# Upper halves of 30 weight tiles of a decoder layer: from ScalarE's rounding to a rounding transfer of GpSimd's

## The chip, the cores and the metric

The kernel runs on one core of a Trainium2 chip. The metric is the device time of one execution in microseconds (us), as a median of several runs. Engines are TensorE (PE), VectorE (DVE), ScalarE (ACT), GpSimd (POOL) and SyncE (SP); each works through its own instructions one after the other in the order in which they stand in the program, and waits at an instruction until what it needs is there.

## What is computed

One layer of a hybrid decoder, on x of 512 positions by 1024 channels, in float32. Cut to what matters:

```python
proj = rmsnorm(x, norm_gain) @ w_in
aq, ak, av, ag, bq, bf, bi, bg, gate_a, gate_b = split(proj)      # 8 of 512 columns, 2 of 1024
ya = moba_attention(rmsnorm(aq), rmsnorm(ak), av, rel_bias)      # 8 heads of 64
ya = (ya * silu(ag)) @ w_up_a
log_f = log_sigmoid(bf) + log1p(lb * exp(min(-bf, 30)))
kb = (1 - lb) * sigmoid(-bf)
yb = rmsnorm(hgrn2_chunkwise(silu(bq), kb, bi, log_f))           # 4 heads of 128
yb = (yb * silu(bg)) @ w_up_b
h = x + (sigmoid(gate_a) * ya + sigmoid(gate_b) * yb) @ w_out
out = h + (p @ w_ple) * sigmoid(h @ w_ple_gate)
```

The input projection is by far the largest product. The attention works on four pairs of heads, the recurrence on four heads.

## The kernel before

**Products in three passes.** A float32 product is made from halves: each operand v is held as an upper half, v rounded to the format fp32r that TensorE multiplies, and a lower half, the rest v − upper, and the product is upper·upper + upper·lower + lower·upper (`mm3`, lines 289 to 295). A weight tile of 128 partitions by 1024 columns holds 8 blocks of 128 channels for 128 outputs, so one tile is 24 matmuls into one PSUM bank.

**Weights.** `w_sequence` lists all weight tiles in the order of use. For each tile `w_load` (lines 258 to 267) brings the raw floats from DRAM to `wf`; from tile 10 on GpSimd issues these transfers (line 266). `w_split` makes the upper half `wh` on ScalarE (line 276), and the lower half `wl` on VectorE (line 277), which reads the raw tile and the upper half. `weight` (lines 280 to 287) is called where a tile is used and lets loads and splits run two tiles ahead. There are two raw buffers, three of `wh` and three of `wl` (line 97): the upper half of tile i takes the buffer of tile i−3, which is free once TensorE has done that tile; the raw tile i takes the buffer of tile i−2, which is free once VectorE has made that one's lower half.

Tiles 0 to 17 are those of the token-major projections and of the first head's `bf` and `bq`. Tiles 18 to 47 are the 30 of `w_tr`, 1024 columns each: the gates `bg` (recurrence) and `ag` (attention), the forget gate `bf` and the query `bq` of recurrence heads 1 to 3, and the merge gates `ga` (gate_a) and `gb`. The ones that are spoken of below: 18 is `bg0`, 19 `ag0`, 20 `bf1`, 21 `bq1`, 22 `bg1`, 23 `ag1`, 26 `bq2`, 25 `bf2`, 32 `bf3`, 37 `ag3`, 39 `ga1`. Behind them come the up-projections (narrower tiles), `w_o` and `w_g`.

**Order.** TensorE's instructions stand in the order of the code, written by hand (`ENG`). In the first part of the kernel those of ScalarE, VectorE and SyncE do too; from the attention on a scheduler places them by its own estimates of when each is ready, and with it the rows of GpSimd's queue.

**Banks.** PSUM has eight banks: three (`mm`) go round among the products of `mm3`, the outputs of the attention and the third score tile of a step; three (`a`) hold scores; two (`g`) serve the recurrence (line 102). A product can begin when what was in its bank three `mm` uses earlier has been read. What reads them last is VectorE: `silu_block` multiplies the gate by its sigmoid (L491, `bg0s` to `bg3s` and `ag0s` to `ag3s`); `hgrn_gates` computes the recurrence's decays from `bf` (L512 to L523, the last a scan over four pieces) and multiplies the query with its sigmoid (L526, the last read of `bq`); `softmax` adds the position bias to the scores and takes their maximum (L832, on `s00x`, `s20x` and so on for a third score tile in an `mm` bank), then ScalarE takes the exponential (L834), VectorE the reciprocal of the sum (L835), ScalarE scales (L836) and VectorE transposes (L839). SyncE then sorts the transposed blocks by transfers (L850) and loads the next pair's bias (L880). In `qk_norm` queries and keys are transposed by L759 and pass through DRAM (`kthere`).

Of the kernel before, what the change touches and what calls it, by code (L numbers as in the profile page):

```python
# [14 lines left out]
AF = mybir.ActivationFunctionType  # L15
# [5 lines left out]
KD = D // 128  # L21
# [28 lines left out]
WAIT = 16  # L50
# [18 lines left out]
def hybrid_layer_kernel(  # L69
# [17 lines left out]
    V, A, G, PE = nc.vector, nc.scalar, nc.gpsimd, nc.tensor  # L87
# [11 lines left out]
    def unit(tag, name, dt=F32, shape=(128, 512)):  # L99
        return sb.tile(list(shape), dt, tag=tag, bufs=BUFS[tag], name=name)  # L100
# [132 lines left out]
    wseq, wraw, wtile, wpos, rounds = [], [], [], [0], {}  # L233
    late = []
# [23 lines left out]
    def w_load(upto):  # L258
        while len(wraw) <= min(upto, len(wseq) - 1):
            ap, kn, cols = wseq[len(wraw)]  # L260
            if len(wraw) >= late[0] or len(wraw) in EARLY:
                raw = unit("VV", f"wf{len(wraw)}", shape=(128, 2, 512)).rearrange("p a b -> p (a b)").rearrange(
                    "p (k c) -> p k c", k=kn)
            else:
                raw = unit("w", f"wf{len(wraw)}", shape=(128, kn, cols))
            (G if len(wraw) >= FAR else nc.sync).dma_start(raw, ap)  # L266
            wraw.append(raw)

    def w_split(upto):
        while len(wtile) <= min(upto, late[1] - 1):  # L270
            i = len(wtile)
            w_load(i)
            ap, kn, cols = wseq[i]
            hi = unit("wh", f"wh{i}", R, (128, kn, cols))
            lo = unit("wl", f"wl{i}", R, (128, kn, cols))
            rounds[i] = A.activation(hi, wraw[i], AF.Copy)  # L276
            V.tensor_tensor(lo, wraw[i], hi.bitcast(F32), op=OP.subtract)  # L277
            wtile.append((hi, lo))

    def weight(ap, ahead=LD):  # L280

        i = wpos[0]
        wpos[0] += 1
        assert wseq[i][0] is ap or str(wseq[i][0]) == str(ap), i
        w_load(i + ahead + (LATE if i + ahead + LATE >= late[0] else 0))
        w_split(i + ahead)
        return wtile[i]
# [631 lines left out]
    def start(kp):  # L919

        if kp == 0:
# [23 lines left out]
            load_x(6, KD)  # L945
            x_gain(2, 3)
            w_split(2)
        elif kp == 1:
            x_gain(3, 4)
            x_square(0)  # L950
            x_square(1)
            x_gain(4, 5)
            w_load(4)
            w_split(3)
            x_square(2)
            x_gain(5, 6)
# [23 lines left out]
    ya, yb, qn, kn, sags, sbgs = [], [], [], [], [], []  # L980
# [365 lines left out]
```

## Time and profile before

| | |
|---|---|
| median of 3 runs | 453.32 us (452.07 to 454.05) |
| the profiled execution | 452.42 us, its span 450.6 us |
| TensorE busy | 445.8 us, 99% |
| VectorE busy | 334.6 us, 74% |
| ScalarE busy | 289.7 us, 64% |
| GpSimd busy | 59.9 us, 13% |
| bytes moved | 59.53 MB, 132 GB/s over the span |

A row of groups reads: line of the program, engine, operation, output<-inputs with their shape, x count, then busy us and the mean ns of one, then the idle us of the engine ahead of these instructions and what ended most of it. A timeline row: start and duration in us from the span's start, engine, line, operation, and in brackets the idle time before it with its releaser. A DMA row: KB of one and the us from issue to landing. A row of windows: for each engine the busy time in the window and its instructions, then the granted TensorE clock (1.00 is full), the mean share of the 16 DMA engines that is busy, and GB/s.

### The profile page before, as it was taken

How to read it: one execution, taken by the hardware profiler on the slowest of the kernel's cores; microseconds unless marked ns; L12 is line 12 of the kernel's file. 1: busy time of each engine (PE TensorE's matmuls, PEld its weight loads, DVE VectorE, ACT ScalarE, POOL GpSimd, SP SyncE). 2: the span in 40 equal slices, each digit the busy share in tenths (PEclk: the TensorE clock that was granted, in tenths of full speed). 3: DMA queues.
4: the chain of work that ended last, by engine and by line, in shares of the span. 5: the costliest groups of instructions: out<-in, count | busy, mean ns of one | idle time of the engine just before them, and what ended most of it. 6: DMA issues, size and time to landing. Idle time of an engine off the chain costs nothing.

```text
span 450.6 us, 8536 instructions
## 1 busy us (share of the span) xinstructions
PE 445.8 (99%) x3192; PEld 376.2 (83%) x3192; DVE 334.6 (74%) x682; ACT 289.7 (64%) x561; POOL 59.9 (13%) x97
## 2 busy tenths in 40 slices
PE   9999999999999999999999999999999999999996
PEld 8888888888878888878887888878888888899996
DVE  5869494776899797949857775465479868999844
ACT  5958474746689988979857996784135434555421
POOL 1000100000000101010100000111210103325520
PEclk9999999999999999999999999999999999999999
DMA  8802424168594455171425444265551444312111
GB/s 265 317 1 94 141 93 129 48 219 197 167 215 127 159 134 178 46 203 49 142 93 155 140 135 148 70 197 149 184 173 47 168 145 143 129 47 95 49 47 48
DMA packets 32857, 59.53 MB, mean 132 GB/s; under 512 B 7088, under 2 KB 18736, under 8 KB 32816
## 3 DMA queue, kind: packets, MB, share of 16 engines
q0 software_dynamic: 9056, 32.51, 22.5%
q1 hardware_dynamic: 23616, 26.47, 20.4%
q8 instruction: 25, 0.41, 0.4%
q14 instruction: 16, 0.13, 0.1%
q10 hardware_dynamic: 144, 0.01, 0.0%
HBM read 48.74 MB, written 4.98 MB: 119 GB/s over the span
## 4 chain that ended last, share of the span: by engine, by line
PE 89%; DVE 5%; SPq 2%; DMA 1%; issue 1%; ACT 0%; DVEq 0%
PE h L293 10%; PE g L1210 9%; PE ga L293 9%; PE gb L293 7%; PE ub L293 5%; PE aq L423 5%; PE ak L423 5%; PE ua L293 5%; PE av L423 5%; PE bf L293 5%; PE bi L423 5%; PE bq L293 4%; PE bg L293 4%; PE ag L293 4%; PE pe L293 2%; SPq L850 2%
## 5 line engine op out<-in xcount | busy, mean ns | idle before, releaser
L276 ACT ACTIVATE wh<-wf 128x1024 fp32r<-128x1024 f32 (+1 forms) x70 | 67.0, 958 | 63.2 <-issue 9.8
L277 DVE TENSOR_TENSOR wl<-wf,wh 128x1024 fp32r<-128x1024 f32 (+1 forms) x70 | 76.8, 1097 | 38.0 <-ACT wh L276 35.7
L266 POOL DMA_DIRECT2D wf<-in_w_tr_dram x30 | 15.8, 528 | 170.5 <-DVE wl L277 115.4
L293 PE MATMUL ga<-xh,wh 128*128 128x512 f32 x64 | 25.3, 396 | 0.4 <-DVE bg3s L491 0.4
L293 PE MATMUL gb<-xh,wh 128*128 128x512 f32 x64 | 25.0, 391 | 0.0
L293 PE MATMUL ga<-xh,wl 128*128 128x512 f32 x64 | 24.9, 390 | 0.0
L293 PE MATMUL ga<-xl,wh 128*128 128x512 f32 x64 | 24.9, 389 | 0.0
L293 PE MATMUL gb<-xl,wh 128*128 128x512 f32 x64 | 24.9, 389 | 0.0
L293 PE MATMUL h<-mh,wh 128*128 128x512 f32 x64 | 24.9, 389 | 0.0
L293 PE MATMUL h<-ml,wh 128*128 128x512 f32 x64 | 24.9, 389 | 0.0
L293 PE MATMUL h<-mh,wl 128*128 128x512 f32 x64 | 24.9, 389 | 0.0
L293 PE MATMUL gb<-xh,wl 128*128 128x512 f32 x64 | 24.9, 389 | 0.0
L834 ACT ACTIVATE pb<-pb,ps 128x128 f32<-128x128 f32 (+3 forms) x32 | 17.6, 551 | 10.0 <-DVE ps L832 10.0
L832 DVE CUSTOM_DVE_ANT_0 pb<-s,bias 128x128 f32<-128x128 f32 (+3 forms) x28 | 12.8, 493 | 7.1 <-DMA bias<-in_ed_dram 4.8
L1187 ACT ACTIVATE sg<-sg 128x256 f32<-128x256 f32 x12 | 5.0, 414 | 20.2 <-DVE sg L1184 20.2
L836 ACT ACTIVATE pb<-pb,ps 128x128 f32<-128x128 f32 (+3 forms) x32 | 16.0, 550 | 0.0
L542 ACT ACTIVATE hx<-hx 128x512 f32<-128x512 f32 x24 | 14.9, 623 | 1.4 <-DVE hx L541 1.3
L266 POOL DMA_DIRECT2D wf<-in_w_up_dram x16 | 8.6, 538 | 52.2 <-DVE wl L277 32.2
L839 DVE STREAM_TRANSPOSE pb<-pb 128x512 f32<-128x512 f32 x20 | 13.8, 696 | 2.0 <-ACT pb L836 2.0
L266 POOL DMA_DIRECT2D wf<-in_w_tok_dram x8 | 4.4, 549 | 80.2 <-DVE wl L277 68.2
L293 PEld LDWEIGHTS ga<-xh,wh 128*128 128x128 f32 x64 | 12.0, 188 | 3.5 <-DVE bg3s L491 0.8
L293 PEld LDWEIGHTS ga<-xh,wl 128*128 128x128 f32 x64 | 12.0, 188 | 2.6
(958 smaller groups left out, 1434.9 us busy)
## 6 DMA issues: line engine op xcount, KB each, us to landing
wf<-in_w_tr_dram POOLq DMA_DIRECT2D x30, 512.0 KB, 4.2
wf<-in_w_tok_dram POOLq DMA_DIRECT2D x8, 512.0 KB, 3.6
wf<-in_w_up_dram POOLq DMA_DIRECT2D x16, 256.0 KB, 3.0
wf<-in_w_o_dram POOLq DMA_DIRECT2D x8, 512.0 KB, 3.8
wf<-in_w_g_dram POOLq DMA_DIRECT2D x8, 512.0 KB, 3.6
wf<-in_w_tok_dram SPq DMA_DIRECT2D x6, 512.0 KB, 7.6
pb<-pb SPq DMA_DIRECT2D x64, 48.0 KB, 2.9
bias<-in_ed_dram SPq DMA_DIRECT2D x8, 256.0 KB, 4.1
```

The costliest lines, as they stand in the source:

```text
L266: (G if len(wraw) >= FAR else nc.sync).dma_start(raw, ap)
L276: rounds[i] = A.activation(hi, wraw[i], AF.Copy)
L277: V.tensor_tensor(lo, wraw[i], hi.bitcast(F32), op=OP.subtract)
L293: dense.append(PE.matmul(ps, a[:, k, :], b[k], start=(n == 0), stop=(n == tot - 1)))
L423: dense.append(PE.matmul(banks[t], a[:, s_], b[:, kk, :], start=(k == 0 and i == 0), stop=(k == KD - 1 and i == 2)))
L542: A.activation(x, x, AF.Exp)
L832: in_order(V.tensor_tensor_reduce(p_, s_[:, so:so + nk], T[j][:, nk - 1::-1], -1.0, 3e38, OP.add, OP.min, st[:, 0:1]))
L834: A.activation(p_, p_, AF.Exp, bias=st[:, 0:1], scale=-1.0, accum_out=st[:, 1:2])
L836: A.activation(p_, p_, AF.Copy, scale=st[:, 2:3])
L839: V.transpose(z[:, :, b_, :].rearrange("p b (n c) -> p b n c", c=32), pb[:, b_].rearrange("p (n b c) -> p b n c", b=4, c=32))
L850: nc.sync.dma_start(pt[32 * b:32 * b + 32, a], z[32 * a:32 * a + 32, b])
L1210: dense.append(PE.matmul(dst[i], a[:, k], b, start=(m == 0 and i in (1, 6, 5)), stop=(m == 11), skip_group_check=i not in (1, 6, 5)))
```

## The change

For tiles 18 to 47 (`WAIT` is 16, `late[0]` the place of the first `w_o` tile; `kn == KD` leaves out the narrow ones and so what follows tile 47 ahead of `w_o`) the upper half no longer comes from ScalarE reading the raw tile. GpSimd issues a second transfer of the same weights from DRAM, straight into the upper half's buffer, whose type is fp32r, so that the transfer rounds. The raw tile is loaded as before and the lower half is computed as before.

```diff
             hi = unit("wh", f"wh{i}", R, (128, kn, cols))
             lo = unit("wl", f"wl{i}", R, (128, kn, cols))
-            rounds[i] = A.activation(hi, wraw[i], AF.Copy)
+            if WAIT < i < late[0] and kn == KD:
+                G.dma_start(hi, ap)
+            else:
+                rounds[i] = A.activation(hi, wraw[i], AF.Copy)
             V.tensor_tensor(lo, wraw[i], hi.bitcast(F32), op=OP.subtract)
             wtile.append((hi, lo))
```

`rounds[WAIT]`, to which `qk_norm` ties an operation, is that of tile 16 and stays as it was. Lines behind 276 are three higher in the changed kernel: L277 is L280, L491 is L494, L526 is L529, L832 is L835. TensorE's order is the same in both. ScalarE's loses 30 rows. GpSimd's gets 30 transfers `wh`, each waiting for its buffer, with the raw loads between and behind them. VectorE's has the same operations, but the scheduler has moved the `wl` rows back.

On VectorE, at the decays of recurrence head 1 (`hu1`, `ha1`, `hk1`; `kl0` is a key's lower half), before:

```order
L277 TENSOR_TENSOR wl23_1288<-wf23_1285,wh23_1287 128x1024
L512 TENSOR_SCALAR hu1_1324<-bf1_1249 128x512
L231 SCALAR_TENSOR_TENSOR kl0_1134<-ktp_1274,sm_68,kh0_1130 128x512
L515 SCALAR_TENSOR_TENSOR ha1_1320<-bf1_1249,ha1_1320 128x512
L517 TENSOR_TENSOR hk1_1329<-ha1_1320,bf1_1249 128x512
L519 TENSOR_TENSOR ha1_1320<-ha1_1320,hu1_1324 128x512
L523 SCALAR_TENSOR_TENSOR hu1_1324<-onec_86,ha1_1320 128x128 x4
L618 TENSOR_TENSOR hkd1_1750<-hu1_1324 128x384
L277 TENSOR_TENSOR wl24_1344<-wf24_1341,wh24_1343 128x1024
```

and now:

```order
L515 TENSOR_SCALAR hu1_1324<-bf1_1249 128x512
L231 SCALAR_TENSOR_TENSOR kl0_1134<-ktp_1274,sm_68,kh0_1130 128x512
L518 SCALAR_TENSOR_TENSOR ha1_1320<-bf1_1249,ha1_1320 128x512
L520 TENSOR_TENSOR hk1_1329<-ha1_1320,bf1_1249 128x512
L522 TENSOR_TENSOR ha1_1320<-ha1_1320,hu1_1324 128x512
L526 SCALAR_TENSOR_TENSOR hu1_1324<-onec_86,ha1_1320 128x128
L280 TENSOR_TENSOR wl23_1288<-wf23_1285,wh23_1287 128x1024
L526 SCALAR_TENSOR_TENSOR hu1_1324<-onec_86,ha1_1320 128x128 x3
L621 TENSOR_TENSOR hkd1_1750<-hu1_1324 128x384
```

`wl23` stood ahead of the decays and stands between the first scan and the other three now, and `wl24` stands further back.

Shortly behind, on VectorE, the bias is added to the first scores (`s00x` is the third score tile, in an `mm` bank) and the query `ha1` is made from `bq1`; before:

```order
L620 TENSOR_TENSOR hkd1_1750<-hkd1_1750,hk1_1329 128x384
L526 TENSOR_TENSOR ha1_1320<-ha1_1320,bq1_1291 128x512
L543 TENSOR_TENSOR hx1_64_1352<-hk1_1329,hx1_64_1352 128x4x64
L622 STREAM_TRANSPOSE hkt1_1754<-hkd1_1750 128x384
L832 ISA pb_70,ps000_1386<-s000_1364,bias00_1307 128x128
L832 ISA ps000_1386 128x1
L832 ISA pb_70,ps001_1391<-s001_1365,bias01_1309 128x128
L832 ISA ps001_1391 128x1
L832 ISA pb_70,ps010_1396<-s002_1366,bias00_1307 128x256
L832 ISA ps010_1396 128x1
L832 ISA pb_70,ps011_1401<-s00x_1367,bias01_1309 128x256
```

and now:

```order
L835 ISA pb_70,ps001_1391<-s001_1365,bias01_1309 128x128
L835 ISA ps001_1391 128x1
L835 ISA pb_70,ps010_1396<-s002_1366,bias00_1307 128x256
L835 ISA ps010_1396 128x1
L835 ISA pb_70,ps011_1401<-s00x_1367,bias01_1309 128x256
L835 ISA ps011_1401 128x1
L835 ISA pb_70,ps020_1407<-s000_1364,bias00_1307 128x384
L835 ISA ps020_1407 128x1
L835 ISA pb_70,ps021_1413<-s001_1365,bias01_1309 128x384
L835 ISA ps021_1413 128x1
L529 TENSOR_TENSOR ha1_1320<-ha1_1320,bq1_1291 128x512
```

The query's row, the last read of the bank of `bq1`, stood ahead of all the score rows and stands behind them now.

On VectorE in the last score step of the second pair (`s110`, `s111`) with the decays of recurrence head 3; before:

```order
L277 TENSOR_TENSOR wl34_2185<-wf34_2182,wh34_2184 128x1024
L277 TENSOR_TENSOR wl35_2216<-wf35_2213,wh35_2215 128x1024
L832 ISA pb_70,ps130_2231<-s110_2223,bias10_1861 128x512
L832 ISA ps130_2231 128x1
L832 ISA pb_70,ps131_2237<-s111_2224,bias11_1863 128x512
L832 ISA ps131_2237 128x1
L512 TENSOR_SCALAR hu3_2411<-bf3_2188 128x512
L515 SCALAR_TENSOR_TENSOR ha3_2407<-bf3_2188,ha3_2407 128x512
L835 RECIPROCAL ps130_2231<-ps130_2231 128x1
```

and now:

```order
L280 TENSOR_TENSOR wl34_2185<-wf34_2182,wh34_2184 128x1024
L835 ISA pb_70,ps130_2231<-s110_2223,bias10_1861 128x512
L835 ISA ps130_2231 128x1
L835 ISA pb_70,ps131_2237<-s111_2224,bias11_1863 128x512
L835 ISA ps131_2237 128x1
L515 TENSOR_SCALAR hu3_2411<-bf3_2188 128x512
L518 SCALAR_TENSOR_TENSOR ha3_2407<-bf3_2188,ha3_2407 128x512
L280 TENSOR_TENSOR wl35_2216<-wf35_2213,wh35_2215 128x1024
L838 RECIPROCAL ps130_2231<-ps130_2231 128x1
```

`wl35` stood ahead of the score rows and stands between the decays and the reciprocal of the softmax now.

On GpSimd, at tiles 21 to 25; before:

```order
L266 DMA wf21_1207<-in_w_tr_dram 128x1024
L266 DMA wf22_1243<-in_w_tr_dram 128x1024
L266 DMA wf23_1285<-in_w_tr_dram 128x1024
L266 DMA wf24_1341<-in_w_tr_dram 128x1024
L266 DMA wf25_1472<-in_w_tr_dram 128x1024
```

and now:

```order
L266 DMA wf21_1207<-in_w_tr_dram 128x1024
L266 DMA wf22_1243<-in_w_tr_dram 128x1024
L277 DMA wh21_1209<-in_w_tr_dram 128x1024
L277 DMA wh22_1245<-in_w_tr_dram 128x1024
L266 DMA wf23_1285<-in_w_tr_dram 128x1024
L277 DMA wh23_1287<-in_w_tr_dram 128x1024
L266 DMA wf24_1341<-in_w_tr_dram 128x1024
L277 DMA wh24_1343<-in_w_tr_dram 128x1024
L266 DMA wf25_1472<-in_w_tr_dram 128x1024
```

Each upper half's transfer stands in the queue ahead of the raw load of the next tile or the one after it.

## Prediction

> **What bounds the kernel now.** I read the page's busy totals first, then its costliest groups, then the busy time of each engine in the stretch where the 30 changed tiles are used, then what ends the waits. From the page:
>
> ```profile
> PE 445.8 (99%) x3192; PEld 376.2 (83%) x3192; DVE 334.6 (74%) x682; ACT 289.7 (64%) x561; POOL 59.9 (13%) x97
> ...
> L276 ACT ACTIVATE wh<-wf 128x1024 fp32r<-128x1024 f32 (+1 forms) x70 | 67.0, 958 | 63.2 <-issue 9.8
> L277 DVE TENSOR_TENSOR wl<-wf,wh 128x1024 fp32r<-128x1024 f32 (+1 forms) x70 | 76.8, 1097 | 38.0 <-ACT wh L276 35.7
> L266 POOL DMA_DIRECT2D wf<-in_w_tr_dram x30 | 15.8, 528 | 170.5 <-DVE wl L277 115.4
> ```
>
> TensorE is busy 99% of the span of 450.6 us. VectorE idles 35.7 us ahead of its `wl` operations because the upper half is not there yet: so the upper half's arrival already paces VectorE. The stretch of the changed tiles, and the twelve us of it that are fullest:
>
> ```profile
> core 0: us, PE busy (x) PEld busy (x) DVE busy (x) ACT busy (x) POOL busy (x), PEclk, DMA share, GB/s
> 107.00:300.00 193.00, 192.60 (x1665) 158.92 (x1663) 147.32 (x361) 157.93 (x339) 16.94 (x32) 1.00 0.49 140
> 124.00:136.00 12.00, 12.00 (x65) 9.66 (x64) 11.69 (x28) 9.81 (x20) 1.06 (x2) 1.00 1.12 218
> ```
>
> TensorE misses 0.40 us in 193, at a granted clock of 1.00. So whatever ScalarE gives back can be worth 0.40 us at most, while anything that makes TensorE wait is paid in full. TensorE's order is written by hand and the same in both kernels, so the question is whether its operands and its PSUM banks still come in time.
>
> The price of a transfer in place of ScalarE's operation has no row, as no transfer of before rounds. The nearest rows are GpSimd's plain loads of the same 512 KB, here from issue to landing: the two loads issued at 108.0 and 109.3; then those issued between 118 and 140 with their landing times; one transfer of SyncE's that they meet; and the landing times of 140 to 185, 185 to 256 and 256 to 300.
>
> ```profile
> wf<-in_w_tr_dram POOLq DMA_DIRECT2D x1, 512.0 KB, 3.5
> wf<-in_w_tr_dram POOLq DMA_DIRECT2D x1, 512.0 KB, 4.4
> L266 POOL DMA_DIRECT2D wf<-in_w_tr_dram x3: 527/527/530, 122.0 to 132.0; - x3
> DMA to landing us min/median/max: 6.6/6.9/10.8
> pb<-kthere SPq DMA_DIRECT2D x3, 256.0 KB, 9.0
> DMA to landing us min/median/max: 3.5/3.6/4.1
> DMA to landing us min/median/max: 3.6/4.8/5.9
> DMA to landing us min/median/max: 2.7/4.3/6.4
> ```
>
> A load lands after 3.5 us where it is alone and after 6.6 to 10.8 us while the attention's key layout passes through DRAM.
>
> **What it removes.** Of ScalarE's 70 roundings 30 go. The others of 1024 columns cost the same 1.05 us or so (rows below), so some 31 us of ScalarE's 157.93 in the stretch. ScalarE is not the bound; all of it lies beside TensorE's work, and the gain ends at the 0.40 us above. Below, the sum has −0.4 for it.
>
> **What it adds.** 30 issues of GpSimd's (30 x 0.528 = 15.8 us on an engine busy 16.94 in 193: nothing by itself), and 30 x 512 KB, as many bytes again as the raw loads, on DMA engines that are busy 0.49 of this stretch: on average it fits. What is late is each single upper half. Its old form began when the tile's buffer was free and ended 1.05 us on; its new form begins at the same moment (the buffer is that of the tile three places earlier, released by TensorE) and lands 3.6 to 4.8 us on in the quiet stages, so each is 2.5 to 3.7 us later. The new issue waits on GpSimd's queue, and the next raw load is queued behind it.
>
> The tile's own matmuls can bear that. One tile in the chain of waits:
>
> ```profile
> 243.36 5.74 PE ga L293 x24
> ```
>
> A buffer freed by the end of tile i−3 leaves two such tiles, some 11 us, until tile i. What can't is VectorE: a `wl` operation waiting there holds all that stands behind it, and behind it stand the operations that free TensorE's banks (L832 on the third score bank, L491 on the gates, L526 on the query). The sum is made at those places.
>
> **A: the first head's attention (the `ag` product of tile 23, at 136.08).** Rows of ScalarE, VectorE and TensorE:
>
> ```profile
> 123.04 1.06 ACT L276 ACTIVATE wh<-wf 128x1024 fp32r<-128x1024 f32 x1 [2.47 <-PE bf L293]
> ...
> 118.08 1.30 DVE L759 STREAM_TRANSPOSE pb<-pb 128x512 f32<-128x512 f32 x2
> ...
> 128.77 1.37 DVE L523 TENSOR_TENSOR_SCAN hu<-onec,ha 128x128 f32<-128x128 f32 x4
> 130.51 1.22 DVE L277 TENSOR_TENSOR wl<-wf,wh 128x1024 fp32r<-128x1024 f32 x1
> 133.12 0.68 DVE L526 TENSOR_TENSOR ha<-ha,bq 128x512 f32<-128x512 f32 x1
> 135.28 0.42 DVE L832 CUSTOM_DVE_ANT_0 pb<-s00x,bias 128x256 f32<-128x256 f32 x1
> ...
> 136.08 0.39 PE L293 MATMUL ag<-xh,wh 128*128 128x512 f32 x1
> ```
>
> Tile 23's upper half can't be fetched before 123.0, when TensorE releases its buffer. Its raw load goes out just before: `wl21` now stands behind the two transposes that end at 119.4, so it ends at 119.4 + 1.1 = 120.5 or later, and raw 23 goes at 121 to 122. From 122.0 to 132.0 + 6.9 = 138.9 three loads took 16.9 us together, 5.6 us each. Two such from 122 end at 133.3 (VectorE's `wl23` then ends at 134.5). Behind `wl23` until the end of `s00x`'s L832 there is, by the rows, 129.1 to 135.70 = 6.6 us, less 1.13 for `wl24` and 0.6 for L526, which both moved back: 4.87. So the bank is free at 134.5 + 4.87 = 139.4 and not before 136.08: **+3.3**. It is nothing if the half lands by 130.1 (6.8 after its issue, the middle of the landing row) and 8 if raw 24, also in flight, takes its share first (133.3 + 5.6 = 138.9).
>
> **B: the next forget gate (`bf2`, at 146.96).** It needs the bank that L491 on `bg1` frees:
>
> ```profile
> 145.85 0.68 DVE L491 TENSOR_TENSOR bg1s<-bg1s,bg 128x512 f32<-128x512 f32 x1
> 146.96 0.39 PE L293 MATMUL bf<-xh,wh 128*128 128x512 f32 x1
> ```
>
> The margin was 146.96 − 146.53 = 0.43. VectorE is 3.7 late from A (139.4 against 135.70) and does L526 in between as well, 0.6: the bank comes 4.3 later, TensorE is 3.3 later: 4.3 − 0.43 − 3.3 = +0.6, if `wl24` and `wl25` find their halves. Six transfers of tiles 23 to 25 at 5.6 us from 122 would end only at 155.6, and with 1.2 for `wl25`, an estimated 2 for the three transposes between (two take 1.30 above) and 0.7 for L491 the bank would come at 159.5 against 146.96 + 3.3 = 150.3: +9.2. After 140 loads are quick again (3.6), so a quarter of the way from 0.6: **+2.8** (0 to 9).
>
> **C: the second head's round (its `ag`, and `bf3` at 194.88).**
>
> ```profile
> 191.42 0.68 DVE L491 TENSOR_TENSOR bg2s<-bg2s,bg 128x512 f32<-128x512 f32 x1
> 194.88 0.39 PE L293 MATMUL bf<-xh,wh 128*128 128x512 f32 x1
> ```
>
> Margin 194.88 − 192.10 = 2.8; two `wl` with a wait stand in the chain ahead of it, each 2.5 later: 5.0 − 2.8 = **+2** (0 to 4).
>
> **D: the third (`ag3` at 231.89, `ga1` at 243.36).** The chain of waits runs from an upper half to `ga1` without slack; two rows of it, then the timeline's rows:
>
> ```profile
> 200.29 1.07 ACT wh L276
> ...
> 204.43 0.60 DVE ha L515
> ...
> 204.95 0.15 DVE L835 RECIPROCAL ps<-ps 128x1 f32<-128x1 f32 x1
> 230.77 0.42 DVE L832 CUSTOM_DVE_ANT_0 pb<-s20x,bias 128x256 f32<-128x256 f32 x1
> 231.89 0.40 PE L293 MATMUL ag<-xh,wh 128*128 128x512 f32 x1
> 243.36 0.50 PE L293 MATMUL ga<-xh,wh 128*128 128x512 f32 x1 [0.40 <-DVE bg3s L491]
> ```
>
> `wl35` moves from ahead of the score rows to between L515 and that reciprocal. Its half's buffer is free at 200.3, so it ends at 200.3 + 4.8 + 1.2 = 206.3, or 207.4 with the longest landing, 5.9: the softmax goes on 1.4 to 2.5 later. `ag3` had 231.89 − 231.19 = 0.7 to spare and takes the rest, `ga1` had nothing to spare and takes it whole, so 1.9 by the middle, and somewhat more, as the chain's loads now run beside twice the weight traffic: **+2.5** (1.4 to 5).
>
> **E: the fourth (`ga3` to `ga5`, 256 to 300).** The landing is 4.3, each half 3.2 later; the margins there are of the size of C's and less. One us at each of two places: **+2** (0 to 4).
>
> **Sum.** 3.3 + 2.8 + 2 + 2.5 + 2 − 0.4 = +12.2. The profiled execution took 452.42 (span 450.6 and 1.8 around it), so 464.6; the median of the runs shown, 453.32, is 0.9 above it: **465.5**. All of the sum's terms take a rounding transfer at a plain one's speed.
>
> **A rule beside it.** The rows say 3.5 us in quiet and 6.6 to 10.8 in the crowd. The Trainium skill, "DMA: Bandwidth & Descriptors", section "Anatomy of one DMA — SWDGE (gpsimd) path", puts one such transfer at about 2.0 us and its bytes by 436 GB/s, an estimate of 3.2 us for 512 KB. The quiet rows agree (3.5); the crowd's don't. By that rule alone every upper half would be in time, which is the first rival's case.
>
> **The rivals.**
>
> *Hidden: not slower (0.10).* The upper halves land early enough everywhere; the point is 6.8 us at A, and about 3.5 at D. With 3.5 (the quiet row): A 123.3 + 3.5 = 126.8 and no wait; B's 0.6 goes with A's delay; C 2.4 under its margin of 2.8; D 200.3 + 3.5 + 1.2 = 205.0, where the reciprocal stood at 204.95: 0; and ScalarE's relief −0.4. Together 452.0 in the profile, 452.9 as the median. For it: the DMA engines are half idle (0.49). Against it: the 9.0 and 10.8 of the crowd at A, and the 4.8 at D. That includes a gain over 0.5%, which the 0.40 us rules out but for 0.01.
>
> *The rounding transfer is itself slower (0.24).* The engines that move the bytes would also change them, and no row shows the price. With twice the landing of the plain one (7.2 to 9.6 in the quiet stages) each half is another 3.6 to 4.8 later, and at the seven places (`ag1`, `bf2`, `ag2`, `bf3`, `ag3`, `ga1`, `ga3`) nothing is left of the margins: 7 x 4.2 = 29 more, 464.6 + 29 = 493.6 and 494.5 as the median. A quarter of that price gives 473. A gain from it is excluded: it reads as many bytes as the plain load.
>
> *The forecast (0.66):* 457 to 475, from A to E with their ends.
>
> **How the numbers follow.** 0.5%, 2.3 us, is about what a measurement of this kernel can tell from no change. Faster by more: 0.01. Within: the hidden case's 0.10 less that 0.01, and 0.01 for the low ends of A to E together: 0.10. Slower: 0.89. The range goes from 455 (the hidden case left out) to 500 (a transfer at twice the time held), which leaves out 0.10 below and some 0.07 above.
>
> **What would show it.** In the changed kernel's profile, TensorE's idle time in 107 to 300 should be some 12 us and not 0.40, put down to VectorE's L835 on `s00x` and `s20x`, L494 on `bg1s`, `bg2s`, `bg3s` and L529 (the same operations, three lines on), with VectorE waiting for the `wh` transfers at its `wl`. ScalarE should be some 31 us less busy. The landing of the `wh` transfers decides: 3.5 to 5 in quiet and about 10 at 123 is the forecast; 7 and more in quiet is the second rival; under 6.8 at 123 the first. I would be wrong in kind if TensorE waited for `wh` or `wl` of its own tile, or if it idled as little as before.

## The result, and the profile after

The changed kernel takes 458.12 us (455.80 to 458.41, 4 runs) against 453.03 for the kernel before (452.07 to 454.05, 4 runs): a ratio of 1.0101 with a 95% interval of 1.0061 to 1.0141, some 5 us slower. Measured again beside experiments 13 to 15 it was 457.79, a ratio of 1.0116 (1.0092 to 1.0139). The prediction said +12.2, with a range from 455 to 500: the sign was right, the size more than double. The ratios leave out executions that took over 1.5% longer than the fastest of their kernel (the medians given do not), and as the profiled execution of run 17 is one of these, only that run's times are used.

The page and the stretch of the changed tiles, with the same columns as before:

```profile
PE 447.7 (98%) x3192; PEld 376.6 (83%) x3192; DVE 333.9 (73%) x682; ACT 261.7 (57%) x531; POOL 76.5 (17%) x127
...
L280 DVE TENSOR_TENSOR wl<-wf,wh 128x1024 fp32r<-128x1024 f32 (+1 forms) x70 | 77.9, 1112 | 50.4 <-DMA wh<-in_w_tr_dram 36.2
...
wf<-in_w_tr_dram POOLq DMA_DIRECT2D x30, 512.0 KB, 4.2
wh<-in_w_tr_dram POOLq DMA_DIRECT2D x30, 512.0 KB, 4.9
```

```profile
core 0: us, PE busy (x) PEld busy (x) DVE busy (x) ACT busy (x) POOL busy (x), PEclk, DMA share, GB/s
107.00:300.00 193.00, 188.54 (x1634) 155.07 (x1633) 144.03 (x352) 127.05 (x296) 30.76 (x58) 0.99 0.71 210
124.00:136.00 12.00, 11.93 (x63) 9.27 (x62) 10.71 (x27) 7.24 (x17) 1.91 (x4) 1.00 1.12 312
```

ScalarE is 28 us less busy, as it should be. The new transfers land nearly as plain ones do (4.9 us against 4.2 in the median of all, 4.8 against 4.6 in 185 to 256). VectorE's idle time ahead of its `wl` operations has grown from 38.0 to 50.4 us; in this stretch its waits for the upper half come to 35.2 us, for the transfers, where they came to 21.2, for ScalarE. TensorE misses 193 − 188.54 = 4.46 us in this stretch and not 0.40, and is busy 1.9 us longer over the span. That is the whole difference of the spans, 456.2 − 450.6 = 5.6, to within 0.4.

Where it waits, in the order of size (engine, line and what for; us, times, longest):

```profile
PE o L866 <- DMA bias<-in_ed_dram: 3.2, 2, 2.8
...
PE bf L296 <- DVE bg1s L494: 0.7, 1, 0.7
PE lpa L566 <- issue: 0.4, 1, 0.4
```

The long one is at the output `o` of the second pair of heads. The name beside it is that of the last transfer on SyncE's queue; what the output needs by the program is the softmax's blocks, sorted by the 16 transfers ahead of it (L853). The chain of waits shows how they became late, then the same place on VectorE's timeline; the third fence is where SyncE began that sorting in the kernel before.

```profile
199.41 0.49 POOL wf L266
199.93 6.21 DMA wh<-in_w_tr_dram
...
206.26 1.23 DVE wl L280
...
217.73 0.51 SPq L853
...
233.12 1.96 PE o L866 x16
```

```profile
206.26 1.23 DVE L280 TENSOR_TENSOR wl<-wf,wh 128x1024 fp32r<-128x1024 f32 x1 [7.14 <-DMA wh<-in_w_tr_dram]
209.82 1.22 DVE L280 TENSOR_TENSOR wl<-wf,wh 128x1024 fp32r<-128x1024 f32 x1
210.95 0.16 DVE L838 RECIPROCAL ps<-ps 128x1 f32<-128x1 f32 x1
```

```profile
212.99 10.98 SPq L850 DMA_DIRECT2D pb<-pb  x16
```

`wl34` waits 7.1 us for its half. That half's transfer stands behind raw load 35 on GpSimd's queue. The load goes at 199.4, once VectorE has made `wl33`; the half's transfer goes at 199.9 and lands 6.2 us later. The reciprocal comes at 210.95 where it came at 204.95, and the sorting begins 4.7 us later than before.

That lateness alone hardly makes TensorE wait. The last sorting transfer is issued 5.4 us later than before (227.8 against 222.4), and it also takes 4.9 us to land and not 2.8, so it lands some 7.5 us later. Before, it had landed some 3.4 us ahead of the matmuls that need it (225.2 against 228.6), and TensorE is itself 1.6 us late here: 5.0 us to spare against 7.5. The wait is 2.8. By estimate, with the old landing time it would have been 0.4; late halves and a slower transfer meet at this place.

Most of the 1.9 us of longer busy time is at one place, right behind that wait:

```profile
232.00:233.00 1.00, 0.00 (x0) 0.00 (x0) 0.47 (x1) 0.00 (x0) 0.00 (x0) 0.95 0.76 287
233.00:234.00 1.00, 0.89 (x9) 0.92 (x11) 0.96 (x3) 0.01 (x1) 0.00 (x0) 0.50 0.07 25
234.00:235.00 1.00, 1.00 (x11) 0.68 (x8) 0.93 (x7) 1.00 (x5) 0.53 (x1) 0.50 0.00 0
235.00:236.00 1.00, 1.00 (x76) 0.99 (x77) 1.00 (x7) 1.00 (x5) 0.00 (x0) 0.50 0.57 184
236.00:237.00 1.00, 1.00 (x43) 0.97 (x36) 1.00 (x9) 1.00 (x5) 0.00 (x0) 0.84 0.88 336
```

The granted clock (third number from the end) is 0.50 for some 3.3 us. In the repeat of the same kernel (run 16) the wait is 1.4 us, the clock stays at 1.00, and the span is 454.7. The products from 222.46 to `ag3` at 237.86 keep TensorE busy for 12.57 us here and for 11.23 in the repeat, so the half clock costs some 1.3 us. The rest of the longer busy time is spread; the repeat is busy 1.5 us longer than the kernel before without any such stretch. The output's matmuls, here and then in the repeat:

```profile
228.75 1.53 PE L866 MATMUL o<-pb,avv 128*64 128x128 f32 x24
233.11 1.97 PE L866 MATMUL o<-pb,avv 128*64 128x128 f32 x16 [2.83 <-DMA bias<-in_ed_dram]
```

```profile
230.18 1.53 PE L866 MATMUL o<-pb,avv 128*64 128x128 f32 x24
233.11 1.09 PE L866 MATMUL o<-pb,avv 128*64 128x128 f32 x16 [1.40 <-DMA bias<-in_ed_dram]
```

The blocks come at the same time in both. The repeat waits 1.43 us less because TensorE had lost 1.43 us more before it got there.

### The profile page after: what moved, and what is told of

The parts are those of the page before. It is cut to its first block, busy times and chain, and to the rows that moved or that the text cites. A ratio compares the mean times of both kernels' runs of the same rounds, so it can differ in the third digit from the quotient of the medians.

```text
span 456.2 us, 8558 instructions
## 1 busy us (share of the span) xinstructions
PE 447.7 (98%) x3192; PEld 376.6 (83%) x3192; DVE 333.9 (73%) x682; ACT 261.7 (57%) x531; POOL 76.5 (17%) x127
## 4 chain that ended last, share of the span: by engine, by line
PE 71%; issue 16%; DMA 4%; POOL 3%; DVE 3%; SPq 2%; POOLq 0%; DVEq 0%
PE ga L296 10%; PE h L296 10%; PE g L1213 9%; PE ub L296 5%; PE aq L426 5%; PE ua L296 5%; PE av L426 5%; PE ak L426 4%; PE bi L426 4%; DMA wh<-in_w_tr_dram 3%; PE gb L296 2%; PE pe L296 2%; SPq L853 2%; POOL wf L266 2%; POOL wh L277 2%
## 5 line engine op out<-in xcount | busy, mean ns | idle before, releaser
L280 DVE TENSOR_TENSOR wl<-wf,wh 128x1024 fp32r<-128x1024 f32 (+1 forms) x70 | 77.9, 1112 | 50.4 <-DMA wh<-in_w_tr_dram 36.2
L279 ACT ACTIVATE wh<-wf 128x1024 fp32r<-128x1024 f32 (+1 forms) x40 | 35.5, 887 | 45.9 <-PE ub L296 11.0
L277 POOL DMA_DIRECT2D wh<-in_w_tr_dram x30 | 16.0, 535 | 63.4 <-PE ag L296 13.6
L835 DVE CUSTOM_DVE_ANT_0 pb<-s,bias 128x128 f32<-128x128 f32 (+3 forms) x28 | 12.9, 494 | 2.4 <-PE s L818 1.1
L296 PEld LDWEIGHTS gb<-xh,wl 128*128 128x128 f32 x64 | 12.0, 188 | 2.5
```

Source lines behind the costliest of these rows:

```text
L277: G.dma_start(hi, ap)
L296: dense.append(PE.matmul(ps, a[:, k, :], b[k], start=(n == 0), stop=(n == tot - 1)))
L835: in_order(V.tensor_tensor_reduce(p_, s_[:, so:so + nk], T[j][:, nk - 1::-1], -1.0, 3e38, OP.add, OP.min, st[:, 0:1]))
```

## The experiments

Each kernel ran beside the kernel before on the same chip. Losses in us are the ratio's excess times 453. Only that of the change itself, 5.1, is the difference of the medians; by its ratios it is 4.6 (2.8 to 6.4) in the first measurement and 5.3 (4.2 to 6.3) in the second. Theories came and went; they are named as the expectations name them.

**1 to 4: which tiles?** The condition alone is edited, from the changed kernel:

```diff
-            if WAIT < i < late[0] and kn == KD:
+            if WAIT < i < late[0] and kn == KD and i not in (34, 35):   # 1
+            if i in (34, 35):                                           # 2
+            if WAIT < i < 32:                                           # 3
+            if 32 <= i < late[0] and kn == KD:                          # 4
```

> Tiles 34 and 35 get their upper halves from ScalarE again, the other 28 by the rounding transfer. Chain theory: the loss is made at one place, the last score step of the second pair, where VectorE waits 7.1 us for the half of tile 34, so that the sorted blocks reach TensorE 2.8 us late and its clock is then halved; with 34 and 35 from ScalarE that wait goes, about 453.0 to 454.5 (0.7 us of the wait at the second forget gate may stay) and no wait of over 1 us of TensorE's. Traffic theory: the loss is that of 15.7 MB more on the DMA engines, spread over many places; 28 of 30 transfers stay, so about 457.5.

> Only tiles 34 and 35 get their upper halves by the rounding transfer, the other 28 from ScalarE. Chain theory, with the margin of some 3 us that the sorted blocks had before: the half of 34 comes about 5 us after its buffer is free, VectorE is 2 to 3 us late there and the margin takes it, about 453.0 to 454.5. A rival chain theory, in which these two tiles alone do it: 456 to 458 with TensorE's one long wait kept. Traffic theory: 2 of 30 transfers, 453.3.

> The rounding transfer for tiles 18 to 31 only (14 of the 30). Chain theory: VectorE's lag of 4 us by 186 us into the span arises here, and the wait of 0.7 at the second forget gate; the long wait needs tile 34's transfer as well and is not there: 453.3 to 454.8. Traffic theory: 14 of 30 of the loss, 455.4.

> The rounding transfer for tiles 32 to 47 only (16 of the 30). Chain theory: without the lag from the earlier tiles the halves of 32 to 35 make the sorted blocks 3 to 5 us late against a margin of 3: 453.0 to 456, a wait of 0 to 2 us at the second pair's output and less than the whole of the 5.1. Traffic theory: 16 of 30 of the loss, 455.7.

Measured: (1) 458.64, ratio 1.0135 (1.0102 to 1.0168), +6.1; (2) 454.49, 1.0038 (1.0016 to 1.0060), +1.7; (3) 459.72, 1.0151 (1.0121 to 1.0181), +6.8; (4) 453.95, 1.0033 (1.0018 to 1.0048), +1.5. The chain theory falls: without tiles 34 and 35 nothing is gained. The traffic theory, in which all bytes count alike, does no better: run 3 should have taken 455.4 by it and run 4 455.7. TensorE's waits moved. In run 3, by the profile:

```profile
PE ag L296 <- DVE ps L835: 2.8, 2, 2.3
PE bf L296 <- DVE bg1s L494: 1.4, 1, 1.4
PE ga L296 <- DVE bg3s L494: 0.9, 1, 0.9
...
PE o L866 <- DMA bias<-in_ed_dram: 0.6, 1, 0.6
```

These are the places of the prediction's terms A, B and D. `ag1` waits 0.6 and `bf2` 1.4, less than forecast; D's two places, `ag3` with 2.3 and `ga1` with 0.9, lose 3.2 together, more than the 2.5 that were forecast. And 14 tiles cost as much as all 30 (+6.8 with 5.5 to 8.2, against 4.6 with 2.8 to 6.4). Two things can make it so, and these four runs don't part them: what a place costs depends on what TensorE has lost before it, and the scheduler puts VectorE's rows elsewhere (in run 3 `wl35` stands ahead of the score rows again).

**5 to 8: the place, the bytes, the buffers.** Runs 5 and 6 edit the condition again. Run 7 is the kernel before with a second transfer behind each raw load, into DRAM. Run 8 is the changed kernel with one more buffer.

```diff
+            if WAIT < i < 26:                                           # 5
+            if 26 <= i < late[0] and kn == KD:                          # 6
...
+            loaded = (G if len(wraw) >= FAR else nc.sync).dma_start(raw, ap)            # 7
+            if WAIT < len(wraw) < late[0] and kn == KD:
+                behind(G.dma_start(scratch.tile([128, kn, cols], F32, tag="dm", name=f"dm{len(wraw)}"), ap), loaded)
...
-    BUFS = {"w": 2, "wh": 3, "wl": 3, "A": 16,
+    BUFS = {"w": 2, "wh": 4, "wl": 3, "A": 14,                          # 8
```

> The chain theory has fallen: without tiles 34 and 35 the time stayed. New theory, late halves: what costs is the stretch where queries and keys pass through DRAM; there an upper half lands 5 to 10 us after TensorE has freed its buffer, and VectorE, waiting for it, frees TensorE's banks late. Here only tiles 18 to 25 come by the rounding transfer. Late halves: most of the loss, 456 to 459, with waits at the tiles 19, 23 and 25. Traffic theory (all bytes count alike): 8 of 30 of the loss, 454.

> Only tiles 26 to 47 come by the rounding transfer. Late halves: 453.5 to 455, as with 32 to 47, no wait of TensorE's before 170. Traffic theory: 22 of 30 of the loss, 456.5.

> Every upper half comes from ScalarE as in the kernel before; behind each raw load of tiles 18 to 47 GpSimd issues a second transfer of the same 512 KB, from DRAM to DRAM, that nobody waits for. So the bytes read and the issues are those of the change, without its waits. Late halves: 452.5 to 454.5. Traffic theory: 457 or more.

> The changed kernel with four buffers for upper halves in place of three (and 14 in place of 16 of the small tiles called A, for the room): the buffer of tile i is free a tile, 5.4 us, earlier, and the transfer with it. Late halves: the loss goes, 452.2 to 454. Traffic theory: the bytes are the same, 457 to 458.

Measured: (5) 456.39, 1.0085 (1.0066 to 1.0105), +3.8; (6) 455.22, 1.0066 (1.0042 to 1.0090), +3.0; (7) 462.91, 1.0188 (1.0155 to 1.0221), +8.5; (8) 463.03, 1.0251 (1.0222 to 1.0280), +11.4. Run 5 came out as late halves foretold, run 6 between the two forecasts. Run 7 was a miss for late halves as the only cause: no half is late in it, VectorE's rows stand nearly as in the kernel before, and it is slower than the change. TensorE's longest wait in it is at the first pair's output:

```profile
PE o L865 <- DMA pb<-pb: 4.5, 1, 4.5
```

The sorting for that output begins 1.6 us later than before (167.5 against 165.9), and those of its transfers that are issued behind 170 land after 4.9 us and not 2.7. Run 8 was a miss as well; it stays hard to read, as it moved many of VectorE's rows, and its control (run 10) is not neutral. Runs 5 and 6 together, 6.8, are more than the whole change, but by no more than the intervals leave open.

**9 to 12: bytes without lateness.** Run 9 is run 7 with an SBUF tile as the target, for which two small buffers were taken away; run 10 is the kernel before with these two away and nothing else. Run 11 is the changed kernel with `wl25` behind the row that frees the bank of `bg1`. In run 12 GpSimd rounds from the raw tile.

```diff
+                behind(G.dma_start(unit("dm", f"dm{len(wraw)}", shape=(128, kn, cols)), ap), loaded)   # 9, with "A": 14, "dm": 1
...
-    BUFS = {"w": 2, "wh": 3, "wl": 3, "A": 16,
+    BUFS = {"w": 2, "wh": 3, "wl": 3, "A": 14,                          # 10
...
+            if i == 25:                                                 # 11
+                behind(low, marks["bg1"])
...
-                G.dma_start(hi, ap)
+                G.tensor_copy(hi, wraw[i])                              # 12
```

> As the run with the bytes alone, but the second transfer of each tile goes into a spare SBUF tile, like the change's, and not back to DRAM (14 small tiles called A in place of 16, for the room). Every upper half comes from ScalarE, so no half is late. Shared engines theory (the extra bytes slow the 48 KB transfers of SyncE that sort the attention's blocks, and TensorE waits for those at the outputs of the pairs): 455.5 to 459, with waits at the pairs' outputs. Late halves theory: 452.5 to 454.5. Both causes: in between, 454.5 to 456.

> The kernel before with 14 small tiles called A in place of 16 and nothing else: the control of the two runs that needed the room. Both theories: 452.5 to 453.8.

> The changed kernel with one pair of rows on VectorE in the other order: the lower half of tile 25 stands behind the multiplication that frees the bank of bg1, not ahead of it. Transfers and bytes are the same. Late halves theory: the wait at the second forget gate (0.7 us in the changed kernel's profile, 1.0 to 2.8 in those of the other runs) shrinks to that for the tile's own lower half, 0 to 0.5: 456 to 457.5. Shared engines theory: 458.

> GpSimd rounds the 30 upper halves itself, from the raw tile, with no second transfer: no byte more than before, but the half comes later than ScalarE's, by estimate 1 to 3 us (GpSimd's additions of 256 columns take 0.86 us in the profile before). Late halves theory: 454.5 to 459, with TensorE's waits at the same places (ag, bf of the second head, the outputs). Shared engines theory: 452.5 to 454.

Measured: (9) 461.63, 1.0179 (1.0148 to 1.0210); (10) 454.50, 1.0049 (1.0027 to 1.0071); (11) 458.05, 1.0100 (1.0068 to 1.0132); (12) 453.24, 1.0014 (0.9996 to 1.0031). The bytes alone cost 1.0179 against 1.0049, some 5.9 us, more than any of the expectations had, and TensorE waits at an output: of run 9, then of its control,

```profile
PE o L865 <- DMA pb<-pb: 4.7, 1, 4.7
```

```profile
PE o L863 <- DMA pb<-pb: 1.9, 1, 1.9
```

The control was expected to be neutral and is not: with two small tiles fewer its sorting begins at 170.9 in place of 165.9, and the output waits even without the extra bytes. So the 5.9 us are the price where there is no margin left. In the change the same output waits 0.4, and the bytes can have cost less there.

The sorting transfers, 48 KB each, take longer to land when 512 KB loads go beside them. From the pages of before, of the change and of run 9:

```profile
pb<-pb SPq DMA_DIRECT2D x64, 48.0 KB, 2.9
```

```profile
pb<-pb SPq DMA_DIRECT2D x64, 48.0 KB, 4.0
```

```profile
pb<-pb SPq DMA_DIRECT2D x64, 48.0 KB, 4.1
```

In run 11 the wait at `bf2` is gone as expected, and the time is the same, as the shared engines theory had it: the waits at the outputs are longer in its place (1.6 and 2.4 us). Run 12 is no slower than the kernel before, which shows, to within 0.8 us, that moving the rounding off ScalarE is worth nothing here and costs nothing. VectorE's rows moved in it too, and at the second pair's last score step `wl35` stands behind the first reciprocal and not ahead of the score rows: with halves in time, TensorE doesn't wait at that output. Run 12 was meant to make the halves late, and my estimate of 1 to 3 us was a miss:

```profile
L277 POOL CAST wh<-wf 128x1024 fp32r<-128x1024 f32 x30 | 35.9, 1198 | 72.5 <-DMA wf<-in_w_tr_dram 24.8 <-PE bq L296 8.8 <-PE ag L296 8.7
```

GpSimd takes 1.2 us for it, hardly more than ScalarE's 1.05. So lateness by itself was still untested.

**13 to 17: lateness without bytes, and where the bytes hurt.** In run 13 the raw loads of tiles 18 to 47 bring an eighth of the tile, and the lower halves are made from that eighth, so they leave out the rest of the weights. Runs 14 and 15 are run 9 for some tiles. Run 16 is the change again. Run 17 is run 13 with `wl23` and `wl24` tied to the places that they have in the changed kernel.

```diff
+            if WAIT < len(wraw) < late[0] and kn == KD:                 # 13
+                G.dma_start(raw[:, 0:1], ap[:, 0:1])
...
+            few = WAIT < i < late[0] and kn == KD
+            V.tensor_tensor(lo, wraw[i][:, 0:1].to_broadcast([128, kn, cols]) if few else wraw[i], hi.bitcast(F32), op=OP.subtract)
...
+            if WAIT < len(wraw) < 26:                                   # 14
+            if 26 <= len(wraw) < late[0] and kn == KD:                  # 15
...
+            if i == 23 and first:                                       # 17, besides 13
+                behind(wlow[i], first[0])
...
+                    if (hp, qb, j) == (0, 0, 0):
+                        behind(wlow[24], inverse)
```

> The changed kernel with an eighth of each raw load of tiles 18 to 47 (64 KB in place of 512): the lower halves of these tiles are made from that eighth and are not those of the reference, the instructions are the same. So the rounding transfers, their waits and VectorE's rows stay, and the bytes are about those of the kernel before. Shared engines theory: the loss goes, 452 to 454, though the halves land 3.5 to 5 us after their buffers are free. Late halves theory: 456 to 458, as the halves are still later than ScalarE's.

> The run with the bytes to a spare SBUF tile, for tiles 18 to 25 only; its control is the kernel with 14 small tiles, 454.5. Shared engines theory with the harm done where the key layout and the raw loads of tiles 18 to 25 meet: 457 to 460. If the harm is done to the sorting transfers behind 150 us: 454.5 to 456.

> The run with the bytes to a spare SBUF tile, for tiles 26 to 47 only; control 454.5. If the harm is done to the sorting transfers behind 150 us: 457.5 to 461, with waits at the pairs' outputs. If it is done by tiles 18 to 25: 454.5 to 456.

> The changed kernel once more, beside these runs on one chip. All theories: 456.5 to 459; its profile shows which of the waits come in every execution and which in some.

> As the run with an eighth of the raw loads (lower halves of tiles 18 to 47 not those of the reference), with VectorE's rows put back where the changed kernel has them: the lower half of tile 24 behind the first reciprocal and not ahead of the score rows. Bytes about those of the kernel before, late halves and waits those of the change. Shared engines theory (the 5.1 us are the extra bytes' doing): 452.5 to 454. Late halves theory: 456 to 458. Both: the time says how the 5.1 divide.

Measured: (13) 463.14, 1.0224 (1.0185 to 1.0262), +10.1; (14) 456.29, 1.0092 (1.0058 to 1.0126); (15) 460.81, 1.0180 (1.0160 to 1.0199); (16) 457.79, 1.0116 (1.0092 to 1.0139); (17) 457.96, 1.0091 (1.0061 to 1.0122), +4.1.

Run 14 came out between the two forecasts, run 15 as the sorting's forecast. Against the control, 1.0049, the bytes of tiles 18 to 25 cost some 1.9 us, those of 26 to 47 some 5.9, as much as all of them: most of the harm is done behind 150 us. That it is done to the sorting is argued from run 15's longest wait, 3.9 us at an output, from the sorting in run 7, and from the landing times above. The intervals are wide: that of the 1.9 reaches down to nearly nothing.

Run 13 was a surprise: the bytes are back to about those of the kernel before, and it loses twice what the change loses. Two rows of its timelines, of VectorE and of TensorE, say why:

```profile
140.53 1.22 DVE L284 TENSOR_TENSOR wl<-wf,wh 128x1024 fp32r<-128x1024 f32 x1 [3.96 <-DMA wh<-in_w_tr_dram]
```

```profile
143.42 0.79 PE L300 MATMUL ag<-xh,wh 128*128 128x512 f32 x1 [6.93 <-DVE ha L533]
```

That is term A of the prediction at full size, and more. The scheduler, seeing shorter loads, had put `wl24` ahead of the score rows; it waits there for a half whose transfer goes at 129.5, and the query's row behind it, for which `ag1` waits, comes late. Run 17 differs from run 13 in the place of `wl24` (and of a few rows beside it) and is 6 us faster. So the place of one of VectorE's rows can decide what a late half costs, and in the changed kernel that place is a mild one. With it, late halves without more bytes cost 4.1 us.

What follows: late halves alone cost 4.1 us (run 17), extra bytes alone some 5.9 (run 9 against 10), and the change, which has both, 5.1 to 5.3. Each is a cause by itself, and they do not add. Without either (run 12) the loss is 0.6, with an interval that holds zero. How the change's own 5 us divide between the two was not settled: taking either away leaves most of the loss, and at the change's longest wait both were needed. Run 9 is also not the change's traffic to the letter, since its second transfers wait for nothing but their queue.

## Why the prediction was wrong in size

**The bound.** Right: 0.40 us was all that could be gained, and TensorE's waits are paid in full. Run 12 confirms that ScalarE's relief is worth nothing.

**The price of a rounding transfer.** Right: nearly that of a plain one (4.9 and 4.2 us in the median, 3.6 and 3.5 at the least in 185 to 256). The rival of a slower one, at 0.24, is out, and with it the upper half of the range. The other rival, that the transfers are hidden, is out as well: `wl34` waits 7.1 us.

**A, +3.3: the first step that failed.** `ag1` doesn't wait in the profile; in the repeat it waits 0.3 us, in runs 1, 3, 5 and 11 between 0.3 and 0.8. What stands between the end of `wl23` and the free bank was right: 4.87 us forecast, 4.91 measured. The landing was not. The prediction divided 16.9 us by three loads and let tile 23's raw load and its half take 5.6 us each, one behind the other, until 133.3. But GpSimd had sat idle 13.9 us ahead of those three loads, waiting for VectorE's `wl` rows, so their spacing was no measure of what the DMA engines can move. In the changed kernel these engines moved 312 GB/s in 124 to 136, where they had moved 218. The half, issued at 122.7, landed 6.7 us later, at 129.4: just ahead of the 130.1 up to which the prediction itself saw no wait. (The term's upper end should read 8.9 by its own steps, not 8.) Run 13, with `wl24` moved ahead, shows the mechanism at 6.9.

**B, +2.8.** Right place (`bf2` behind L494 on `bg1`), 0.7 in the profile and 0.9 in the repeat. The quarter of the way toward the crowded price was too much; it rests on the same 5.6 us. That the lower end, 0.6, came out is luck: it stood for VectorE being late from A, which it wasn't. What made the bank late is `wl25`, which waited 1.9 us for its half.

**C, +2, and E, +2.** `bf3` does not wait. Its bank came 4.1 us later than before, where 5.0 were forecast; there were 2.8 to spare, and TensorE was itself 1.6 late. 0.4 us are lost at the first pair's output, and 0.4 behind 256. Little of either.

**D, +2.5.** The chain was right and its end was wrong. `wl35` was to end at 206.3 to 207.4 and ends at 211.0, since `wl34` is late as well: the prediction took the buffer's release as the start of each transfer, though the order rows for tiles 21 to 25 had raw loads ahead of halves on GpSimd's queue, as here. The chain then doesn't run out at `ag3` or `ga1` but at the output before them, through SyncE's sorting, which the prediction's chain of waits passed through and to which it gave no term. There 2.8 us are lost, and the half clock behind it, some 1.3 us, had no term either. That 2.8 is close to the term's 2.5 is luck.

**The other step that failed is the sum.** B alone took off what TensorE had lost before, at A. C, D and E were set against the margins of before and then added. But TensorE late at one place has that much more room at the places behind it, as far as the other engine's work doesn't itself wait for TensorE. Run 16 beside the change showed this above, 1.43 us for 1.43. At `ag3` and `ga1` the banks came 3.9 us later than before and TensorE 6.0 and 5.4 later, so nothing waits there, though `ga1` had no margin before. By the prediction's own numbers C is nothing once A and B stand: 5.0 late, against 2.8 to spare and 6.1 lost. Carried along so, A and B alone remain, 6.1 − 0.4 = +5.7, close to what was measured, but by luck, as most of the time went elsewhere.

The parts of the change show it too: 6.8 (18 to 31) and 1.5 (32 to 47), or lateness and bytes, 4.1 and 5.9, against 4.6 to 5.3 for the whole. These differences are more than the intervals allow; that of 3.8 (18 to 25) and 3.0 (26 to 47) is not. Each part has its own order of VectorE's rows, so not all of this need be the adding.

**What the prediction passed over** with the words "on average it fits" is what happens beside the new transfers. The share of the DMA engines rose from 0.49 to 0.71, and it does fit on average; but the small transfers on the softmax's chain land later (2.9 to 4.0 us in the median), and in runs 7 and 9 this costs as much by itself as the lateness does in run 17.

## What to carry to other kernels

Delays on one engine's path are not simply added up: walk through the places in order, carry the engine's own lateness along, and charge each place only with what exceeds it. The spacing of loads in a trace is a rate of the DMA engines only if the loads were issued without waiting for another engine. A transfer that doubles the bytes is priced twice, by its own landing and by what it does to the small transfers beside it that sit on a chain. And where a scheduler sets the order, an edit moves rows: before the time of an experiment is read, compare its order with that of the kernel it came from (run 13 against 17, 6 us for one row's place).

## What the runs showed of the hardware that was not expected

A wait of TensorE's of some 2.4 us or more is often, not always, followed by about 3.3 us at a granted clock of 0.50. It followed waits of 2.39 (run 11), 2.52 (run 1) and 2.83 us (the change). It did not follow waits of 1.4 (the repeat), 2.27 (run 3) and 2.38 us (run 7), nor one of 2.84 us in run 8. So the length of the wait alone does not decide it. Behind two longer waits, 4.5 us in run 7 and 6.9 in run 13, the clock stayed at 0.50 for some 6.8 us. In the change one such stretch costs some 1.3 us, which is one reason why executions of one kernel differ (455.8 us at a mean clock of 0.999, 458.4 at 0.996; but also 458.2 at 0.998). The Trainium skill, "TensorE: Matmul & The Clock Gate", section "Part 1: The HAM clock gate (the "warmup" mystery)", has the half rate set in after at least one idle window of about 3.4 us. The measured 0.50 is that half rate, and the 3.3 us that it holds are about one such window; but the three waits of under 3 us that led to it were shorter than one. The section also says that the window runs freely and doesn't start anew with the kernel, which would let waits of one length go either way, as those of 2.83 and 2.84 us do.

GpSimd's own copy rounds a 128 x 1024 tile in 1.2 us on average, so near ScalarE's 1.05 that it could stand in for it.
